# A mixture-of-experts decoder layer on one core: experts placed by token count, 14 of 32 places with 64 slots and two passes over the weights

## The chip, the cores and the metric

The kernel runs on one core of a Trainium2 chip (trn2). The metric is the device time of one execution in microseconds; lower is better. TensorE (PE) multiplies matrices; VectorE (DVE), ScalarE (ACT) and GpSimd (POOL) do the other arithmetic; SyncE (SP) issues most DMA transfers, which run on the core's 16 DMA engines. Every engine works through its own instructions in program order and meets the others at semaphores.

## The reference

One decoder layer for 512 tokens of width 1024, all in float32. Retention, dilated attention and their merge come first and are the same in both kernels. What matters here is the mixture of experts at the end: a softmax router picks 4 of 32 experts for each token, and an expert is a clamped SwiGLU network with weights of 1024 x 2048 and 1024 x 1024.

```python
logits = xf @ w_router + b_router
top_val, top_idx = lax.top_k(logits, 4)
gates = softmax(top_val)
# for each expert e, on the tokens that chose it (xb):
u = xb @ w1[e] + b1[e]
glu = minimum(u[:, ::2], 7.0)
lin = clip(u[:, 1::2], -7.0, 7.0)
a = glu * sigmoid(1.702 * glu) * (lin + 1.0)
y = a @ w2[e] + b2[e]                 # added to the token's row, times its gate
```

The weights of all experts are 32 x 12 MB. 512 x 4 choices over 32 experts are 64 tokens per expert in the mean.

## The kernel before

The mixing half fills the first part of the program. Then the router: for each of four blocks of 128 tokens, `choose` finds the four experts, `count` and `rank` give each token its place in its expert's list (`rk1`), and `gates` writes the gate as three bfloat16 parts into `aux`, beside the token's number.

The expert stage takes the experts in order, e = 0 to 31, each with 96 slots (`CAP`). Weights come as tiles of 1 MB: eight "A" tiles for the first matrix (128 rows of 2048 columns) and four "B" tiles for the second. The list `tiles` has the order: A tiles of e, then the B tiles of e - 1. `load` (L847) issues a tile's DMA from SP into a ring of 11 buffers (`NRA` + `NRB` + `NRC`). A float32 product is made of reduced-precision ones (float32r): `prep_hi` (L1010) has ACT round a weight tile into `w_hi`, `prep_lo` (L1016) has DVE subtract that from the weights into `w_lo`, and then issues the load that reuses the tile's buffer. There are four buffers for `w_hi` and four for `w_lo`, and both run `AHEAD` = 3 tiles ahead of the matmuls in program order. The activations are split the same way into `xh`, `xl`, 96 columns each. A tile then takes three groups of four matmuls, xh by hi, xh by lo, xl by hi, each with 512 columns (L1217 for A, L1232 for B):

```python
for s_, m_ in ((xh, hi), (xh, lo), (xl, hi)):
    for j in range(4):
        PE.matmul(U[e][:, j], s_[:, k], m_[:, j * 512:(j + 1) * 512], start=False, ...)
```

The order of everything else is written out by hand in the loop over `tiles`, at fixed tile numbers k of A(e). `slot_hot` (k = 5, DVE, L1098) and `slot_sum` (k = 7, PE) find the tokens of expert e + 2; `slot_rows` (ACT and POOL) makes their numbers and gathers the rows with an indirect DMA (L1119). `turn` (PE, L1130) transposes the gathered rows of e + 1 at k = 5 and 6, and the activations of e - 1 at k = 3 and 4; `turn_copy` (L1075 ACT, L1076 DVE) splits them. `evacuate`, at the first two B tiles that follow A(e), reads the sums u: `open_gates` (ACT, L1141), `linear` (DVE, L1146), `times_glu` (DVE, L1150). `times_gate` (DVE, L1153) follows at k = 1 of the next A, and `finish` at k = 0 of the one after it: DVE scales y into `ys` (L1158), POOL adds the rows to `s_acc` in HBM with an indirect DMA (L1159). u is one PSUM buffer of four banks, y one of two, so A(e + 1) can't begin before u of e is read. Biases enter by a matmul each (`bias_mm`, L1094).

`overflow_list` writes down which experts have more than 96 tokens; after the 32 places a loop on the chip (L1281) takes one extra pass for each such block. The final norm follows.

Of the kernel before, what the change touches and what calls it, by code (L numbers as in the profile page):

```python
# [27 lines left out]
CAP = 96  # L28
F2 = 2048
# [6 lines left out]
NRB = 2  # L36
# [14 lines left out]
def _constants():  # L51
# [30 lines left out]
    m = np.zeros((P, 324), np.float32)  # L82
# [6 lines left out]
    m[:, 259] = np.arange(P) % 32  # L89
    for p in range(P):  # L90
        m[p, 260 + 32 * (p // 64) + p % 32] = 1.0
# [5 lines left out]
def body(tc, a, out):  # L97
# [14 lines left out]
    misc = cp.tile([P, 324], F32, name="misc")  # L112
# [668 lines left out]
    G.tensor_copy(sel, misc[:, 260:324].rearrange("p (a b) -> p a b", a=2))  # L781
# [65 lines left out]
    loaded, his, los = {}, {}, {}  # L847
# [54 lines left out]
    def choose(t):  # L902
# [29 lines left out]

    def gates(t0, t1):
# [7 lines left out]
        g0, g1 = gt[:, 0, :n], gt[:, 1, :n]  # L941
# [150 lines left out]
    def bias_mm(ps, e, r):  # L1092
        c = (r % 3) * 512
        PE.matmul(ps, sel[:, r // 3, e:e + 1].to_broadcast([P, CAP]), btile[:, c:c + 512], start=True, stop=False)  # L1094

    def slot_hot(rk_e):
        oh = m2.tile([P, NT, CAP], BF, name="oh", bufs=1)
        V.tensor_tensor(oh, iota96[:, None, :].to_broadcast([P, NT, CAP]), rk_e[:, :, None].to_broadcast([P, NT, CAP]),  # L1098
                        op=OP.is_equal)
        return oh  # L1100

    def slot_sum(oh, aux_e):
        ps = psC.tile([CAP, 8], F32, name="psl", tag="pt", bufs=2)
        for t in range(NT):
            PE.matmul(ps[:, :6], oh[:, t], aux_e[:, t], start=(t == 0), stop=(t == NT - 1))
        return ps

    def slot_rows(ps, fetch_rows=True):
        sl = m2.tile([CAP, 10], F32, name="sl")
        A.activation(sl[:, :6], ps[:, :6], AF.Copy)  # L1110
        G.tensor_scalar(sl[:, 6:7], sl[:, 2:3], misc[:CAP, 258:259], misc[:CAP, 257:258], op0=OP.mult, op1=OP.add)  # L1111
        G.tensor_add(sl[:, 7:8], sl[:, 0:1], sl[:, 1:2])
        idx = m2.tile([CAP, 1], I32, name="idx", bufs=4)
# [3 lines left out]
        if fetch_rows:  # L1117
            xg = m2.tile([CAP, D], F32, name="xg", bufs=1)
# [3 lines left out]
        gate = m2.tile([CAP, 1], F32, name="gate", bufs=4)  # L1122
# [21 lines left out]
    def linear(u):  # L1144
        av = m2.tile([CAP, 4, 256], F32, name="av", bufs=1)
# [6 lines left out]
    def times_gate(sg, av):  # L1152
        V.scalar_tensor_tensor(av, sg, top7[:CAP, 1:2], av, op0=OP.min, op1=OP.mult)  # L1153
        return av.rearrange("p a b -> p (a b)")

    def finish(y, gate, idx):
        ys = m2.tile([CAP, D], F32, name="ys", bufs=1)
        V.scalar_tensor_tensor(ys, y.rearrange("p a b -> p (a b)"), gate, gtF[:CAP], op0=OP.mult, op1=OP.mult)  # L1158
        G.indirect_dma_start(out=acc, out_offset=bass.IndirectOffsetOnAxis(ap=idx[:, :1], axis=0), in_=ys,  # L1159
                             in_offset=None, compute_op=OP.add)  # L1160

    def overflow_list():
        pc = psC.tile([E, E], F32, name="pc", tag="pt", bufs=2)
        for t in range(NT):
            PE.matmul(pc, trib[:, 1, :E], selb[:, t], start=(t == 0), stop=(t == NT - 1))
        cn = m1.tile([E, 4, E], F32, name="cn")
        V.tensor_scalar(cn[:, 0], pc, float(CAP), None, op0=OP.is_gt)
        for b in range(2, 6):
# [203 lines left out]
```

## Time and profile before

| | |
|---|---|
| median of 3 runs | 1931.7 us (1931.44 to 1932.92) |
| the profiled execution | 1930.4 us, its span 1928.6 us |
| granted TensorE clock, mean | 0.981 |
| instructions | 23299 |
| loads of weight tiles | 384 of 1 MB, median 8.1 us from issue to landing |
| HBM read, written | 503.35 MB, 19.99 MB |

All times are of one execution taken by the hardware profiler. PE is the row of matmuls, PEld that of weight loads into the array, which overlap matmuls. Matmuls are pipelined, so what counts is the distance from one start to the next, not the length of one. "Idle before" is the time that the engine stood still just before, and behind the arrow stands what ended it. PEclk is the granted share of TensorE's full clock of 2.4 GHz: 0.50 is 1.2 GHz. The letter q behind an engine is its queue of instructions. x12 is a count.

### The profile page before, as it was taken

How to read it: one execution, taken by the hardware profiler on the slowest of the kernel's cores; microseconds unless marked ns; L12 is line 12 of the kernel's file. 1: busy time of each engine (PE TensorE's matmuls, PEld its weight loads, DVE VectorE, ACT ScalarE, POOL GpSimd, SP SyncE). 2: the span in 40 equal slices, each digit the busy share in tenths (PEclk: the TensorE clock that was granted, in tenths of full speed). 3: DMA queues.
4: the chain of work that ended last, by engine and by line, in shares of the span. 5: the costliest groups of instructions: out<-in, count | busy, mean ns of one | idle time of the engine just before them, and what ended most of it. 6: DMA issues, size and time to landing. Idle time of an engine off the chain costs nothing. (4 is left out here: it accounts for less than half of the span.)

```text
span 1928.6 us, 23299 instructions
## 1 busy us (share of the span) xinstructions
PE 1847.5 (96%) x8937; PEld 1381.2 (72%) x8937; DVE 1507.3 (78%) x1489; ACT 1025.8 (53%) x939; POOL 411.9 (21%) x404
## 2 busy tenths in 40 slices
PE   5979999999999979999999999999999999999994
PEld 4868888888778866666766766766766766766662
DVE  7474536567553587999999999999999999999993
ACT  5133323222222336666766766676776676776672
POOL 2140001010110123432222232232232232232201
PEclk8999999999999989999999999999999999999997
DMA  9513334433663848999999999999999999999963
GB/s 313 161 54 101 89 90 141 120 90 94 190 174 110 308 153 319 335 370 366 365 361 373 370 356 373 373 351 379 368 358 367 378 358 369 372 357 373 366 238 104
DMA packets 207650, 524.90 MB, mean 272 GB/s; under 512 B 11974, under 2 KB 127094, under 8 KB 174640
## 3 DMA queue, kind: packets, MB, share of 16 engines
q1 hardware_dynamic: 197024, 492.33, 70.8%
q0 software_dynamic: 10512, 31.06, 6.7%
q8 instruction: 71, 1.16, 0.3%
q14 instruction: 43, 0.35, 0.1%
HBM read 503.35 MB, written 19.99 MB: 271 GB/s over the span
## 5 line engine op out<-in xcount | busy, mean ns | idle before, releaser
L1016 DVE TENSOR_TENSOR w_lo<-w_moe,w_hi 128x2048 fp32r<-128x2048 f32 x384 | 874.6, 2290 | 87.6 <-ACT w_hi L1010 83.7
L1010 ACT ACTIVATE w_hi<-w_moe 128x2048 fp32r<-128x2048 f32 x384 | 736.3, 1918 | 359.8 <-PE u L1217 237.9
L1217 PE MATMUL u<-w_hi,x 128*96 128x512 f32 x2048 | 555.5, 398 | 0.0
L1217 PEld LDWEIGHTS u<-w_hi,x 128*96 128x96 f32 x2048 | 319.1, 162 | 122.2 <-issue 0.5
L1217 PE MATMUL u<-w_lo,x 128*96 128x512 f32 x1024 | 278.2, 393 | 0.0
L1232 PE MATMUL y<-w_hi,at 128*96 128x512 f32 x1024 | 264.5, 396 | 0.0
L1232 PEld LDWEIGHTS y<-w_hi,at 128*96 128x96 f32 x1024 | 165.8, 162 | 72.2 <-ACT at L1075 0.2
L1217 PEld LDWEIGHTS u<-w_lo,x 128*96 128x96 f32 x1024 | 165.1, 161 | 72.0
L1111 POOL TENSOR_SCALAR sl<-sl,misc 96x1 f32<-96x1 f32 x32 | 75.9, 2371 | 502.8 <-ACT sl L1110 502.8
L194 PE MATMUL pp<-hTh,w_hl 128*128 128x512 f32 x400 | 162.1, 405 | 0.0
L195 PE MATMUL pp<-hTl,w_hl 128*128 128x512 f32 x400 | 158.4, 396 | 0.0
L196 PE MATMUL pp<-hTh,w_hl 128*128 128x512 f32 x400 | 158.4, 396 | 0.0
L185 DVE TENSOR_TENSOR w_hl<-w_raw,w_hl 128x1024 fp32r<-128x1024 f32 (+1 forms) x66 | 90.9, 1390 | 74.2 <-ACT w_hl L184 74.2
L1232 PE MATMUL y<-w_lo,at 128*96 128x512 f32 x512 | 140.2, 396 | 0.0
L1159 POOL DMA_INDIRECT s_acc<-ys,idx x32 | 58.3, 1823 | 360.9 <-DVE ys L1158 345.3
L1232 PEld LDWEIGHTS y<-w_lo,at 128*96 128x96 f32 x512 | 83.1, 162 | 36.3
L184 ACT ACTIVATE w_hl<-w_raw 128x1024 fp32r<-128x1024 f32 (+1 forms) x66 | 65.2, 1002 | 73.7 <-PE pp L196 56.2
L194 PEld LDWEIGHTS pp<-hTh,w_hl 128*128 128x128 f32 x400 | 75.4, 188 | 20.1 <-issue 2.2
L196 PEld LDWEIGHTS pp<-hTh,w_hl 128*128 128x128 f32 x400 | 75.3, 188 | 18.4
L195 PEld LDWEIGHTS pp<-hTl,w_hl 128*128 128x128 f32 x400 | 75.4, 189 | 16.6
L259 POOL DMA_DIRECT2D s_mod<-brow x16 | 7.9, 493 | 283.0 <-DVE brow L256 251.9
L226 PE MATMUL pp<-w_hl,hTh 128*128 128x256 f32 x224 | 67.4, 301 | 0.4 <-ACT w_hl L210 0.4
(294 smaller groups left out, 2345.1 us busy)
## 6 DMA issues: line engine op xcount, KB each, us to landing
w_moe<-in_w_mlp SPq DMA_DIRECT2D x384, 1024.0 KB, 8.1
w_raw<-in_w_in SPq DMA_DIRECT2D x76, 512.0 KB, 5.5
w_ada<-in_w_ada SPq DMA_DIRECT2D x24, 1024.0 KB, 5.7
w_raw<-in_w_ret_o SPq DMA_DIRECT2D x8, 512.0 KB, 4.4
w_o<-in_w_o SPq DMA_DIRECT2D x4, 1024.0 KB, 5.1
xin<-in_x SPq DMA_DIRECT2D x4, 512.0 KB, 6.5
w_raw<-in_w_att_o SPq DMA_DIRECT2D x8, 256.0 KB, 4.5
xs<-in_x SPq DMA_DIRECT2D x8, 256.0 KB, 4.8
```

The costliest lines, as they stand in the source:

```text
L184: A.activation(hi[:, :kc], raw, AF.Copy)
L185: eng.tensor_tensor(lo[:, :kc], raw, hi[:, :kc].bitcast(F32), op=OP.subtract)
L194: PE.matmul(ps, hi[:, k], mh[:, k], start=(k == 0), stop=False)
L195: PE.matmul(ps, hi[:, k], ml[:, k], start=False, stop=False)
L196: PE.matmul(ps, lo[:, k], mh[:, k], start=False, stop=(k == kc - 1))
L226: PE.matmul(ps[:, tt], xh, hi, start=(kc == 0), stop=False)
L1010: A.activation(his[i], loaded[i], AF.Copy)
L1016: V.tensor_tensor(los[i], loaded[i], his[i].bitcast(F32), op=OP.subtract)
L1111: G.tensor_scalar(sl[:, 6:7], sl[:, 2:3], misc[:CAP, 258:259], misc[:CAP, 257:258], op0=OP.mult, op1=OP.add)
L1159: G.indirect_dma_start(out=acc, out_offset=bass.IndirectOffsetOnAxis(ap=idx[:, :1], axis=0), in_=ys, in_offset=None, compute_op=OP.add)
L1217: PE.matmul(U[e][:, j], s_[:, k], m_[:, j * 512:(j + 1) * 512], start=False, stop=(k == KC - 1 and s_ is xl))
L1232: PE.matmul(Y[e][:, n], s_[:, 2 * k + c], m_[:, col:col + 512], start=False, stop=(k == 3 and s_ is al and c == 1))
```

## The change

The experts are sorted by their token count on the chip. Experts 0 and 1 keep their places; the other thirty follow in falling order of count, assigned to 18 large places ("L", 96 slots) first and to 14 small ones ("S", 64 slots) after. The places are run in the order `KIND` = "LLLL" + "LS" x 14, so from place 4 on large and small alternate, and the last place is small.

In a small place the high and low parts of the activations lie side by side: 64 + 64 columns are one stationary operand of 128 columns. A weight tile then takes two groups of four matmuls, by hi and by lo, and gives 128 rows of sums: rows 0 to 63 from the high parts, rows 64 to 127 from the low parts. At the end `lower` has ACT copy the lower rows out of PSUM, and `fold` has PE add them to the upper rows, one matmul for each bank against a shifted identity.

The sort is done on PE and DVE during the tiles of expert 0: `sort_counts` at k = 0, `sort_rows` and `sort_turn` at k = 1, `sort_tables` at k = 3. It gives `sorted_i` (which expert is at which place), and `rkp`, `aux` and the selectors of the biases in the order of the places. From place 2 on, SP reads the expert's number from `sorted_i` into a register, and the addresses of the loads come from it. The ring of load buffers has 10 places instead of 11. `evacuate` is done in one step at the first B tile instead of two. `overflow_list` counts by the slots of each place, and the extra loop takes the expert's number from the list.

The diff, cut to its core:

```diff
+SMALL = 64
+KIND = "LLLL" + "LS" * 14
...
-NRB = 2
+NRB = 1
...
+        if kind == "A" and k == 0 and e > 1:
+            which[e] = nc.values_load(sorted_i[0:1, e:e + 1], engines=[mybir.EngineType.SP], min_val=0, max_val=E - 1)
+        at = ds(which[e], 1) if e > 1 else slice(e, e + 1)
         if kind == "A":
-            SP.dma_start(w, dram(w1, (e * D + k * P) * F2, [[F2, P], [1, F2]]))
+            SP.dma_start(w, w1[0, at].rearrange("o (k p) n -> p (o k) n", p=P)[:, k])
         else:
             SP.dma_start(w.rearrange("p (k n) -> p k n", k=2),
-                         dram(w2, (e * D + k * 2 * P) * D, [[D, P], [P * D, 2], [1, D]]))
+                         w2[0, at].rearrange("o (k p) n -> p (o k) n", p=P)[:, 2 * k:2 * k + 2])
...
+        V.tensor_copy(selb[:, t], sel_t[t % 2][:, None, :].to_broadcast([P, 4, E]))
...
+    def gate_parts(g, rest, s):
+        V.tensor_copy(aux[:, :, s, 3], g)
+        V.tensor_tensor(rest, g, aux[:, :, s, 3], op=OP.subtract)
+        V.tensor_copy(aux[:, :, s, 4], rest)
+        V.tensor_tensor(aux[:, :, s, 5], rest, aux[:, :, s, 4], op=OP.subtract)
...
-        V.tensor_tensor(g0, g1, nm[:, 1, :n, None].to_broadcast([P, n, E]), op=OP.mult)
-        V.tensor_copy(aux[:, t0:t1, :, 3], g0)
-        V.tensor_tensor(g1, g0, aux[:, t0:t1, :, 3], op=OP.subtract)
-        V.tensor_copy(aux[:, t0:t1, :, 4], g1)
-        V.tensor_tensor(aux[:, t0:t1, :, 5], g1, aux[:, t0:t1, :, 4], op=OP.subtract)
+        V.tensor_tensor(rg[:, t0:t1, 1], g1, nm[:, 1, :n, None].to_broadcast([P, n, E]), op=OP.mult)
+        if t1 == NT:
+            gate_parts(rg[:, :, 1, 0:2], gt[:, 1, :, 0:2], slice(0, 2))
...
+    def two_parts(t, e):
+        if KIND[e] == "L":
+            t = t.rearrange("p (a k c) -> p a k c", a=2, k=KC)
+            return [t[:, 0], t[:, 1]]
+        both = t[:, :KC * P].rearrange("p (k c) -> p k c", k=KC)
+        return [both[:, :, :SMALL], both[:, :, SMALL:], both]
...
+    def lower(ps):
+        n = ps.shape[1]
+        low = m1.tile([P, 4, 512], F32R, name="low")
+        A.activation(low[SMALL:, :n], ps[SMALL:], AF.Copy)
+        return low
+
+    def fold(ps, low):
+        for j in range(ps.shape[1]):
+            PE.matmul(ps[:SMALL, j], shift[SMALL:], low[SMALL:, j], start=False, stop=True, skip_group_check=True)
...
+    def sort_counts():
+        ps = psC.tile([P, 40], F32, name="cnt", tag="pt", bufs=2)
+        for t in range(NT):
+            PE.matmul(ps[:, 0:1], selb[:, t].rearrange("p a e -> p (a e)"), trib[:, 1, 0:1], start=(t == 0), stop=(t == NT - 1))
+        for t in range(NT):
+            PE.matmul(ps[:, 8:40], trib[:, 1], selb[:, t, 0], start=(t == 0), stop=(t == NT - 1))
+        V.scalar_tensor_tensor(sc_[:, 0:1], ps[:, 0:1], 32.0, misc[:, 264:265], op0=OP.mult, op1=OP.add)
+        V.tensor_copy(sc_[:, 1:2], ps[:, 0:1])
+        V.scalar_tensor_tensor(so[:, 0], ps[:, 8:40], 32.0, misc[:, 299:331], op0=OP.mult, op1=OP.add)
+        V.tensor_scalar(so[:, 1], so[:, 0], sc_[:, 0:1], None, op0=OP.is_gt)
+        V.tensor_reduce(sc_[:, 2:3], so[:, 1], axis=AX.X, op=OP.add)
+        V.tensor_scalar(so[:, 2], misc[:, 267:299], sc_[:, 2:3], None, op0=OP.is_equal)
+        for a_ in range(2):
+            V.tensor_copy(both[E * a_:E * (a_ + 1), a_], so[E * a_:E * (a_ + 1), 2])
+        for a_ in range(2):
+            V.tensor_scalar(sel[:, a_, 2:], so[:, 2, 2:], misc[:, 265 + a_:266 + a_], None, op0=OP.mult)
...
+    def sort_rows():
+        ps = psC.tile([E, 2, E], F32, name="srt", tag="pt", bufs=2)
+        PE.matmul(ps[:, 0], misc[:E, 256:257].to_broadcast([E, E]), so[:E, 2], start=True, stop=True)
+        PE.matmul(ps[:, 1], sc_[:E, 1:2].to_broadcast([E, E]), so[:E, 2], start=True, stop=True)
+        V.tensor_copy(sorted_i, ps[0:1, 0])
+        V.tensor_copy(sq_, ps)
+
+    def sort_turn():
+        ps = psC.tile([2 * E, NT, P], F32, name="rgt", tag="pt", bufs=2)
+        for t in range(NT):
+            PE.transpose(ps[:, t], rg[:, t].rearrange("p a e -> p (a e)"), ident)
+        rgT = m2.tile([2 * E, NT, P], F32, name="rgT", tag="ys", bufs=1)
+        A.activation(rgT, ps, AF.Copy)
+        return rgT
+
+    def sort_tables(rgT):
+        ps = psC.tile([P, NT, 2, E], F32, name="srt2", tag="pt", bufs=2)
+        for t in range(NT):
+            PE.matmul(ps[:, t], rgT[:, t], both, start=True, stop=True)
+        V.tensor_copy(rkp, ps[:, :, 0])
+        V.tensor_copy(rg[:, :, 1], ps[:, :, 1])
+        gate_parts(rg[:, :, 1, 2:], rg[:, :, 0, 2:], slice(2, E))
...
-    def evacuate(e, step):
-        if step == 0:
-            SG[e] = open_gates(U[e])
-            AVS[e] = linear(U[e])
-        else:
-            times_glu(U.pop(e), AVS[e])
+    def evacuate(e):
+        if KIND[e] == "S":
+            fold(U[e], now["low"])
+        u = U.pop(e)[:slots_of(e)]
+        SG[e] = open_gates(u)
+        AVS[e] = linear(u)
+        times_glu(u, AVS[e])
+
+    def close(e):
+        if KIND[e] == "S":
+            fold(Y[e], now["ylow"])
+        finish(Y.pop(e), SL[e][1], SL[e][0])
...
+            if e == 0 and k == 1:
+                sort_rows()
+                rgT = sort_turn()
+            if e == 0 and k == 3:
+                sort_tables(rgT)
...
+            else:
+                for m_ in (hi, lo):
+                    for j in range(4):
+                        PE.matmul(U[e][:, j], X[e][2][:, k], m_[:, j * 512:(j + 1) * 512], start=(k == 0 and m_ is hi),
+                                  stop=False, skip_group_check=True)
+                    if k == 0 and m_ is hi:
+                        for j in range(4):
+                            bias_mm(U[e][:SMALL, j], e, j, False)
...
+            if e == 0 and k == 0:
+                sort_counts()
...
-                finish(Y.pop(e - 2), SL[e - 2][1], SL[e - 2][0])
+                close(e - 2)
...
+            if k == KC - 1:
+                if KIND[e] == "S":
+                    now["low"] = lower(U[e])
+                if e == 0:
+                    evacuate(0)
...
+        else:
+            if e + 1 < E:
+                if k == 0:
+                    evacuate(e + 1)
+                if e + 1 == E - 1 and k == 2:
+                    AVS[e + 1] = times_gate(SG.pop(e + 1), AVS[e + 1])
+                    AT[e + 1] = at_tiles(e + 1)
+            if k == 3:
+                if KIND[e] == "S":
+                    now["ylow"] = lower(Y[e])
+                if e >= E - 2:
+                    close(e)
```

`close` is called for the place before last and the last at the end of their own B tiles. The B tiles of a small place are built like its A tiles, with `AT[e][2]` as the stationary operand.

## Rows read from the trace of the kernel before

**Rows 1.** The page: busy us (share of span), instructions, by engine.

```profile
PE 1847.5 (96%) x8937; PEld 1381.2 (72%) x8937; DVE 1507.3 (78%) x1489; ACT 1025.8 (53%) x939; POOL 411.9 (21%) x404
```

**Rows 2.** Windows, expert stage: us, busy us (count) by engine, PEclk, DMA share, GB/s.

```profile
1100.00:1200.00 100.00, 99.92 (x464) 69.92 (x462) 93.28 (x58) 69.55 (x48) 31.12 (x24) 1.00 1.00 369
```

**Rows 3.** Waits, 900 to 1800 us: waiter, releaser, total us, times, longest.

```profile
ACT w_hi L1010 <- PE u L1217: 180.2, 175, 1.8
...
DVE w_lo L1016 <- ACT w_hi L1010: 60.3, 146, 0.7
```

**Rows 4.** Line 853, a load, 900 to 1800 us: issue to landing.

```profile
DMA to landing us min/median/max: 6.1/8.1/10.9
```

**Rows 5.** Timeline of SP's queue: start us, us, engine, line, operation, names, count.

```profile
971.30 21.00 SPq L853 DMA_DIRECT2D w_moe<-in_w_mlp  x8
...
1007.84 21.01 SPq L853 DMA_DIRECT2D w_moe<-in_w_mlp  x8
```

**Rows 6.** Timeline of PE's weight loads, one B tile, then an A tile.

```profile
1003.42 0.86 PEld L1232 LDWEIGHTS y<-w_lo,at 128*96 128x96 f32 x4
...
1006.20 0.86 PEld L1232 LDWEIGHTS y<-w_lo,at 128*96 128x96 f32 x4
...
1021.96 0.86 PEld L1217 LDWEIGHTS u<-w_lo,x 128*96 128x96 f32 x4
...
1025.08 0.85 PEld L1217 LDWEIGHTS u<-w_lo,x 128*96 128x96 f32 x4
```

**Rows 7.** Timeline of PE's weight loads, stage before the experts.

```profile
691.61 0.19 PEld L833 LDWEIGHTS o<-wo_hl,mg 128*128 128x128 f32 x1
...
691.84 0.19 PEld L834 LDWEIGHTS o<-wo_hl,mg 128*128 128x128 f32 x1
```

**Rows 8.** Groups by shape, one expert (1008.05 to 1044.6): busy us, mean ns, idle before.

```profile
L1016 DVE TENSOR_TENSOR w_lo<-w_moe,w_hi 128x2048 fp32r<-128x2048 f32 x13 | 29.6, 2290 | 2.5 <-ACT w_hi L1010 2.5
...
L1010 ACT ACTIVATE w_hi<-w_moe 128x2048 fp32r<-128x2048 f32 x12 | 23.0, 1918 | 11.1 <-PE u L1217 7.2 <-PE y L1232 2.1 <-DMA w_moe<-in_w_mlp 0.9
...
L1158 DVE SCALAR_TENSOR_TENSOR ys<-y,gate,gtF 96x1024 f32<-96x1024 f32 x1 | 1.3, 1272 | 0.0
...
L1146 DVE TENSOR_SCALAR av<-u 96x1024 f32<-96x1024 f32 x1 | 1.2, 1214 | 0.0
...
L1076 DVE TENSOR_TENSOR x<-pt,x 128x384 fp32r<-128x384 f32 x2 | 1.1, 547 | 0.0
...
L1141 ACT ACTIVATE sg<-u 96x1024 f32<-96x1024 f32 x1 | 1.0, 1001 | 0.0
```

**Rows 9.** Timeline of DVE, start of the first expert.

```profile
714.44 0.27 DVE L944 CAST aux<-gt 128x64 bf16<-128x64 f32 x1
...
716.46 6.69 DVE L1016 TENSOR_TENSOR w_lo<-w_moe,w_hi 128x2048 fp32r<-128x2048 f32 x3
```

**Rows 10.** Timeline of PE: two waits, [idle before <-releaser].

```profile
748.41 1.99 PE L1094 MATMUL u<-btile,selrow 128*96 128x512 f32 x4 [3.84 <-DVE av L1150]
...
1888.20 1.17 PE L1094 MATMUL y<-btile,selrow 128*96 128x512 f32 x2 [4.03 <-DVE ys L1158]
```

**Rows 11.** Windows around them, and one ahead of the first expert.

```profile
747.85:751.26 3.41, 2.85 (x7) 1.99 (x8) 2.61 (x2) 0.00 (x0) 2.82 (x3) 0.50 0.98 359
...
1887.90:1894.73 6.83, 6.53 (x20) 4.60 (x21) 3.08 (x4) 2.78 (x3) 1.43 (x1) 0.50 0.40 59
...
710.30:720.54 10.24, 8.10 (x27) 6.40 (x28) 9.72 (x16) 4.43 (x6) 0.49 (x1) 0.50 0.70 217
```

**Rows 12.** Line 1280: a register read on SP's queue, minimum/median/maximum ns.

```profile
L1280 SPq TENSOR_LOAD <-li x1: 481/481/481, 1862.6 to 1862.6; - x1
...
L1280 SPq FUSED_REGOPS  x1: 181/181/181, 1863.2 to 1863.2; - x1
```

**Rows 13.** A window of 8 us in the expert stage.

```profile
864.00:872.00 8.00, 7.92 (x38) 5.38 (x37) 7.51 (x5) 4.50 (x4) 1.50 (x1) 1.00 1.02 408
```

**Rows 14.** The page, groups: the accumulates of the experts' rows.

```profile
L1159 POOL DMA_INDIRECT s_acc<-ys,idx x32 | 58.3, 1823 | 360.9 <-DVE ys L1158 345.3
```

More of the change, by code (lines that the diff above doesn't have):

```diff
@@ L89, in _constants @@
     m[:, 259] = np.arange(P) % 32
+    e = np.arange(E)
     for p in range(P):
-        m[p, 260 + 32 * (p // 64) + p % 32] = 1.0
+        if p % 32 < 2:
+            m[p, 260 + 2 * (p // 64) + p % 32] = 1.0
+    first = np.where(e == 0, 1e6, np.where(e == 1, 5e5, 0.0)) - e
+    m[:, 264] = first[np.arange(P) % 32]
+    m[:, 265] = np.arange(P) < 64
+    m[:, 266] = np.arange(P) >= 64
+    large = [i for i in range(E) if KIND[i] == "L"]
+    small = [i for i in range(E) if KIND[i] == "S"]
+    rank = np.zeros(E)
+    rank[large + small] = np.arange(E)
+    slots = np.array([CAP if k == "L" else SMALL for k in KIND])
+    m[:, 267:299] = rank[None]
+    m[:, 299:331] = first[None]
+    m[:, 331:363] = slots[None]
+    m[:, 363:394] = np.diff(slots)[None]
     c["k_misc"] = m
@@ L920, in count @@
         for tt in range(t + 1):
-            PE.matmul(pr, trib[:, 0 if tt == t else 1], selb[:, tt], start=(tt == 0), stop=(tt == t))
+            PE.matmul(pr, trib[:, 0 if tt == t else 1], selb[:, tt, 0], start=(tt == 0), stop=(tt == t))
         return pr
@@ L988, in body @@
             load_x(t, n)
+    sorted_i = rt.tile([1, E], I32, name="sorted_i")
     for i in range(NRA + NRB):
@@ L1126, in turn @@
     def turn(rows, q):
+        n = rows.shape[0]
         pt = psC.tile([P, 4, CAP], F32, name="pt", tag="pt", bufs=2)
@@ L1159, in finish @@
+        V.scalar_tensor_tensor(ys, y[:n].rearrange("p a b -> p (a b)"), gate, gtF[:n], op0=OP.mult, op1=OP.mult)
         G.indirect_dma_start(out=acc, out_offset=bass.IndirectOffsetOnAxis(ap=idx[:, :1], axis=0), in_=ys,
                              in_offset=None, compute_op=OP.add)
-    def overflow_list():
[L1163 to L1168, printed above, removed]
-            V.scalar_tensor_tensor(cn[:, 0], pc, float(b * CAP), cn[:, 0], op0=OP.is_gt, op1=OP.add)
+    so = m1.tile([P, 3, E], F32, name="so")
@@ new lines, in body @@
+    sc_ = m1.tile([P, 3], F32, name="sc")
+    sq_ = m1.tile([E, 2, E], F32, name="sq")
+    both = m1.tile([2 * E, 2, E], F32, name="both")
+    G.memset(both, 0.0)
+    def sort_counts():
[14 more added lines that the diff above has]
+            V.tensor_scalar(sel[:, a_, 2:], so[:, 2, 2:], misc[:, 265 + a_:266 + a_], None, op0=OP.mult)
@@ new lines, in sort_tables @@
+    def sort_tables(rgT):
[5 more added lines that the diff above has]
+        gate_parts(rg[:, :, 1, 2:], rg[:, :, 0, 2:], slice(2, E))
+    def overflow_list():
+        cn = m1.tile([E, 5, E], F32, name="cn")
+        V.tensor_sub(cn[:, 4], sq_[:, 1], misc[:E, 331:363])
+        V.tensor_scalar(cn[:, 0], cn[:, 4], 0.0, None, op0=OP.is_gt)
+        for b in range(1, 5):
+            V.scalar_tensor_tensor(cn[:, 0], cn[:, 4], float(b * CAP), cn[:, 0], op0=OP.is_gt, op1=OP.add)
@@ L1211, in body @@
                 U[e] = u_tile()
-                for j in range(4):
-                    bias_mm(U[e][:, j], e, j)
-            xh, xl = X[e]
-            for s_, m_ in ((xh, hi), (xh, lo), (xl, hi)):
-                for j in range(4):
-                    PE.matmul(U[e][:, j], s_[:, k], m_[:, j * 512:(j + 1) * 512], start=False,
-                              stop=(k == KC - 1 and s_ is xl))
+                if KIND[e] == "L":
+                    for j in range(4):
+                        bias_mm(U[e][:CAP, j], e, j)
+            if KIND[e] == "L":
+                xh, xl = X[e]
+                for s_, m_ in ((xh, hi), (xh, lo), (xl, hi)):
+                    for j in range(4):
+                        PE.matmul(U[e][:CAP, j], s_[:, k], m_[:, j * 512:(j + 1) * 512], start=False,
+                                  stop=(k == KC - 1 and s_ is xl))
+            else:
+                for m_ in (hi, lo):
+                    for j in range(4):
+                        PE.matmul(U[e][:, j], X[e][2][:, k], m_[:, j * 512:(j + 1) * 512], start=(k == 0 and m_ is hi),
+                                  stop=False, skip_group_check=True)
+                    if k == 0 and m_ is hi:
+                        for j in range(4):
+                            bias_mm(U[e][:SMALL, j], e, j, False)
         else:
```

175 lines of the change are left out of this document (95 added, 80 removed).

## The prediction

> **What bounds the kernel now.** I read the page first, then the windows, the waits and the expert's own rows. Over the span PE is busy 96% and DVE 78% [rows 1]; the mean hides stages, so the reader should go to 100 us in the middle of the expert stage: PE 99.92, DVE 93.28, ACT 69.55 us, and the DMA engines at a share of 1.00 with 369 GB/s [rows 2]. Three resources look full. The waits tell them apart: ACT's `w_hi` waits for PE to give a buffer back (180.2 us in 900), DVE's `w_lo` waits for ACT (60.3 us) [rows 3], and a load lands 6.1 to 10.9 us after its issue [rows 4], though it is issued eleven weight tiles ahead. So PE sets the pace and the loads are early. One expert lasts 1007.84 - 971.30 = 36.54 us [rows 5], twelve tiles at 3.05, so a load has some 30 us.
>
> Inside it, a tile of 12 matmuls takes 1006.20 - 1003.42 = 2.78 us, 0.2317 us each; a tile with four transposes 1025.08 - 1021.96 = 3.12, so 0.34 for them [rows 6]. 144 + 6 bias matmuls are 34.75 us, four sets of transposes 1.36, and the rest of 36.54, 0.43, is the slot sums.
>
> **The change part by part.** 14 places (e = 5, 7, ... 31; call them S) put the high and low parts of up to 64 tokens side by side as one 128-column stationary. Then two products (hi, lo) replace three: 96 matmuls for 144. Whether 128 columns cost more than 96 shows in the stage before: two weight loads of 128 columns with 512-column matmuls lie 691.84 - 691.61 = 0.23 us apart [rows 7], so no. S adds six `fold` matmuls (four on u, two on y) that contract 64 rows; no row has one. A transpose is 0.09 (0.34 / 4), a 512-column matmul at half clock 0.46; I take 0.2317, the nearest in columns, and the ends are worth 1 us a pair. PE per S place: 108 x 0.2317 + 1.36 + 0.43 = 26.8 us; a pair of L and S 63.3 instead of 73.1.
>
> DVE splits the same weights: 12 `w_lo` at 2.29 us and the vector work on 1024 columns. That takes 1.21 to 1.27 us on 96 partitions, just over half of 2048 columns on 128 [rows 8]: length goes by columns, and 64 partitions save nothing. An L place needs 0.9328 x 36.54 = 34.1 us; in a pair the five small operations of S have a third fewer columns (5 x 0.18 = 0.9 less): 67.3 us. ACT: 25.4 us per L place; S adds `lower`, 2048 columns of u and 1024 of y, 2.0 and 1.0 us by `sg`, which takes 1.00 for 1024 from PSUM [rows 8]; 53.8 per pair. `lower(u)` waits on ACT for the last matmul of k = 7, and behind it stands the `w_hi` of the second B tile: 2.0 + 1.9 us, while DVE still has three `w_lo` (6.7 us) to make, so nobody waits. `fold` stands on PE behind the first B tile and holds the other three for 0.9 us, counted below. So after the change DVE needs more than PE, and the most that a pair can gain is 73.1 - 67.3 = 5.8 us.
>
> It will not get all of that, since the engines follow one program order with four `w_hi` and four `w_lo` buffers. Follow one turn of the loop of waits. `times_gate` of the place before sits on DVE behind `w_lo` of k = 4, and PE can't transpose at k = 3 before it. In an S place PE arrives there early (its first tiles take 1.86 us, DVE's `w_lo` 2.29, and `ys` and `times_gate` stand between), so PE idles. From there PE runs without a stop: five S tiles (40 matmuls), the B tiles of the L place before (50 with bias), the fold of u (4), the next L place's A tiles (100): 194 x 0.2317 = 44.9, eight sets of transposes 2.7, two slot sums 0.9: 48.5 us. At the end of that k = 7 tile a `w_hi` buffer is free: ACT 1.92 us [rows 8]. Then DVE is late: six `w_lo` (three in a row took 6.69 us, 2.23 each [rows 9]) 13.4, the two operations on u at 1.21 and `ys` and `times_gate` at 1.27 [rows 8] (the second of each kind takes the same) 5.0: 18.4 us, to the next `times_gate`. One turn is 48.5 + 1.9 + 18.4 = 68.8 us. L places stay PE-bound, S places become DVE-bound, and the handover costs 1.5 us of the 5.8.
>
> The idle before k = 3 is 5 to 6 us: after the third tile PE has nothing for `w_lo` (2.2), `ys` (1.3) and `times_gate` (1.3) and part of another `w_lo`. The trace has two idle stretches of that kind: PE stands from 744.56 and resumes at 748.41; its granted clock is 0.50 (1.2 GHz) from 747.85 to 751.26. At 1888.20 after 4.03 us it is 0.50 until 1894.73 [rows 10, 11]. So PE runs at half clock for 2.85 and 6.53 us after it resumes and loses 1.4 or 3.3 us. The stretch after the idle is on the turn's path. I take 2.0, nearer to the short case since the idle lies on no other disturbance there; both ends go into the range. A pair then takes 70.8 us and saves 2.3; thirteen pairs (e = 5 to 30) 30 us.
>
> The sort, at the start. `sort_counts`, `sort_rows`, `sort_tables` and the longer `overflow_list` add on DVE about 11 + 2 + 6 + 7 small operations, less about four that `gates` drops there: 22 x 0.2 to 0.27 us, as the small casts there [rows 9], 5 us. On PE some 18 small matmuls and transposes, under 2 us; ACT one copy. In this first expert DVE is late: PE waits 3.84 us for DVE's `av` [rows 10]. So I take nearly all, +4.5; 0 if DVE's slack in the next L places hid it, 8 if PE's new wait for `oh` at k = 1 sets its clock back once more.
>
> The loads: from e = 2 on each address comes from a register. Thirty reads of `sorted_i` on SP's queue; the only such read on SP in the trace takes 0.48 us plus 0.18 of register work [rows 12]. SP issues a load every 3 us at 0.33 us, and a load lands over 20 us before its use, so this hides; were it uncovered, 30 x 0.66 = 20 us. One buffer fewer in the ring (11 to 10) takes about 3 us of that lead: nothing, unless the DMA queue is the limit (a rival). Gather and accumulate move 64 rows for 96. Evacuating u in one step moves `times_glu` one tile earlier, before the next A needs u: nothing.
>
> The end: the last place is S. Its B tiles have 16 matmuls fewer (-3.7 us), with `lower` (1.0) and `fold` (0.5 and handoffs) ahead of the last `ys`, -2; its A tiles save half a pair's gain, -1. Together -3.
>
> The sum goes against the profiled execution, 1930.4 us (span 1928.6; 1.3 below the median of 1931.7): 1930.4 + 4.5 - 30 - 3 = 1902 us.
>
> **The rivals.**
> 1. *DVE alone bounds the pairs*: times_gate's wait is soaked up and PE's clock stays at 1.00. Then 67.3 a pair, 5.8 x 13 = 75: 1930.4 + 4.5 - 75 - 3 = 1857 us. For it: DVE has work all through S. Against: its waits for ACT [rows 3] don't vanish in L places.
> 2. *DMA is at its limit*: share 1.00 at 369 GB/s [rows 2]. A pair moves 73.1 x 369 = 26.97 MB now and 0.26 less after (32 rows x 4 KB, in and out), 72.4 us: 0.7 x 13 = 9: 1922 us. Against it: a window of 8 us in the same stage at 408 GB/s and a share of 1.02 [rows 13], and loads that land 8 us after issue instead of filling their 30 us lead. The pairs as forecast want 26.7 MB in 70.8 us, 377 GB/s, under those 408. Beside it, the Trainium skill ("DMA: Bandwidth & Descriptors", Where 436 GB/s comes from) says that about 358 GB/s of HBM per core binds such loads; by that rule a pair's 25.8 MB of reads would take 72.1 us, a gain of 13 us in all before head and tail, 1919. The window at 408 GB/s speaks against it as a limit here.
> 3. *Slower: PE's clock*. If each S place's idle is followed by a low stretch like that of 10.24 us at 710.30 [rows 11], PE loses 5.1 us a turn: 73.9 a pair, 0.8 x 13 = 10 lost: 1930.4 + 4.5 + 10 - 3 = 1942. It decides from 73.1 - 68.8 = 4.3 us lost, that is 8.6 us at half clock on the path. For it: one such idle comes every pair, and later waits inside S may hold the clock down; against: the two single idle stretches cost 1.4 and 3.3.
> 4. *It doesn't fit*: an S place with over 64 tokens goes to the extra loop, an expert's 12 loads again, at least 36.5 us and nothing hidden: 1902 + 37 = 1939 or more. In the trace the loop never ran: 32 accumulates for 32 experts [rows 14]. From the reference's inputs, experts 0 and 1 get 71 and 54 tokens, the sixteen largest others 66 to 91, the fourteen smallest 40 to 62. So it should fit.
>
> **How the numbers follow.** Forecast 0.57 (own range 1871, no clock loss and no head, to 1922, a clock loss of 3.3 and a head of 8); rival 1 0.13; rival 2 0.12; rival 3 0.13; rival 4 0.05. A measurement of this kernel can tell 0.2%, 4 us, from no change. Faster: nearly all of the forecast, rival 1 and most of rival 2: 0.78. Same: the rest of 2 and the near side of 3: 0.08. Slower: 0.14. The range must take in rival 1's 1857 and rival 2's, and leaves the slower cases out: 1852 to 1932.
>
> **What would show it.** Right: load issues of two places 70 to 72 us apart, the S half shorter than 36.5 and the L half near 36; in S, DVE busy nearly throughout, PE idle 5 us before the transposes of `av` with `times_gate` as releaser, and a granted clock of 0.50 after it; in L, ACT's `w_hi` still waiting for PE. Wrong: `w_hi` waiting for DMA in each pair (rival 2); no clock below 1.00 and 67 us pairs (rival 1); pairs over 73 (rival 3); more than 32 accumulates (rival 4).

## The result: 1909.8 us, 1.2% faster, and the profile after

The changed kernel takes 1909.8 us (median of 4 runs, 1909.71 to 1911.79) where the kernel before took 1932.3 beside it (1931.44 to 1934.36): ratio 0.9884, interval 0.9867 to 0.9902. The profiled execution took 1909.79, its span 1908.0. The forecast was 1902, counted from the profiled 1930.4: 20.6 us were gained where 28.4 were forecast.

The page's engine line and a window of the expert stage, as [rows 1, 2]:

```profile
PE 1754.7 (92%) x8369; PEld 1332.6 (70%) x8369; DVE 1491.2 (78%) x1506; ACT 1052.6 (55%) x968; POOL 463.7 (24%) x406
```

```profile
1100.00:1200.00 100.00, 90.02 (x396) 64.77 (x395) 93.33 (x58) 72.93 (x54) 27.95 (x24) 0.94 1.00 369
```

PE lost ten points in this window, which holds two of its stands (from 1000 to 1100 us, with one, it is busy 95.05); DVE kept its 93, and the DMA row has not moved: the transfers follow the pace of the experts, as e7 below shows. The waits from 900 to 1800 us, as [rows 3], say who is late now:

```profile
ACT w_hi L1039 <- PE u L1339: 109.9, 96, 1.8
...
PEld pt L1175 <- DVE av L1209: 73.3, 25, 5.4
PE pt L1175 <- DVE av L1209: 62.4, 13, 5.0
DVE w_lo L1045 <- ACT w_hi L1039: 59.1, 78, 1.6
```

Thirteen times, once per pair, PE stands ahead of the transposes (L1175) for `times_gate` (L1209). Loads land in a median of 8.1 us as before [rows 4], and 32 accumulates of rows stand in the page as in [rows 14]: no extra pass.

One turn of the loop, in the timeline of one pair (start us, us, engine, line, operation, names, [idle before <-releaser]):

```profile
1483.81 0.90 PE L1175 MATMUL pt<-misc,av 96*128 96x96 f32 x4 [5.00 <-DVE av L1209]
...
1535.40 1.92 ACT L1039 ACTIVATE w_hi<-w_moe 128x2048 fp32r<-128x2048 f32 x1 [1.03 <-PE u L1339]
...
1537.35 2.32 DVE L1045 TENSOR_TENSOR w_lo<-w_moe,w_hi 128x2048 fp32r<-128x2048 f32 x1 [0.71 <-ACT w_hi L1039]
...
1554.18 1.27 DVE L1209 SCALAR_TENSOR_TENSOR av<-sg,top,av 96x1024 f32<-96x1024 f32 x1
...
1555.50 0.90 PE L1175 MATMUL pt<-misc,av 96*128 96x96 f32 x4 [5.01 <-DVE av L1209]
```

PE takes 1535.40 - 1483.81 = 51.59, ACT 1.95, DVE 1555.45 - 1537.35 = 18.10, the handover 0.05: 71.69 us. No row of that chain has idle time inside its part. The clock behind one of the stands (window; PE resumes at 979.94):

```profile
979.94:986.07 6.13, 6.13 (x19) 4.98 (x20) 6.13 (x4) 2.89 (x3) 0.12 (x1) 0.50 1.04 371
```

Where the 20.6 us of the spans went is seen in the start of the first A matmul of a place, beside the kernel before and one more (e8 below: before with its constant tile widened):

```
us                            before   e8 (padded)   after
first A matmul                 718.0      714.7      711.9
places 0 and 1                  70.5       72.6       76.4
A(2)                           788.5      787.3      788.4
A(5)                           899.6      898.2      899.3
A(31)                         1849.3     1845.5     1829.7
13 pairs, A(5) to A(31)        949.7      947.3      930.4
span                          1928.6     1923.4     1908.0
```

Nearly all lies in the pairs: 73.05 became 71.57. A pair has two halves: 39.1 us from the first A matmul of the small place to that of the large one, and 32.6 from there to the next small one.

### The profile page after: what moved, and what is told of

Read it like the earlier page. It is cut to its first block, busy times and chain, and to the rows that moved or that the text cites. A ratio compares the mean times of both kernels' runs of the same rounds, so it can differ in the third digit from the quotient of the medians.

```text
span 1908.0 us, 23014 instructions
## 1 busy us (share of the span) xinstructions
PE 1754.7 (92%) x8369; PEld 1332.6 (70%) x8369; DVE 1491.2 (78%) x1506; ACT 1052.6 (55%) x968; POOL 463.7 (24%) x406
## 3 DMA queue, kind: packets, MB, share of 16 engines
q1 hardware_dynamic: 197024, 492.36, 71.4%
## 5 line engine op out<-in xcount | busy, mean ns | idle before, releaser
L1339 PE MATMUL u<-w_hi,x 128*96 128x512 f32 x1152 | 315.8, 401 | 0.0
L1339 PEld LDWEIGHTS u<-w_hi,x 128*96 128x96 f32 x1152 | 180.3, 163 | 72.1 <-issue 0.2
L1339 PE MATMUL u<-w_lo,x 128*96 128x512 f32 x576 | 156.9, 394 | 0.0
L1364 PE MATMUL y<-w_hi,at 128*96 128x512 f32 x576 | 151.3, 396 | 0.0
L1344 PE MATMUL u<-w_hi,x 128*128 128x512 f32 x448 | 141.1, 440 | 0.0
L1344 PE MATMUL u<-w_lo,x 128*128 128x512 f32 x448 | 130.6, 417 | 0.0
L1364 PEld LDWEIGHTS y<-w_hi,at 128*96 128x96 f32 x576 | 91.7, 161 | 44.4 <-issue 5.9
L1344 PEld LDWEIGHTS u<-w_lo,x 128*128 128x128 f32 x448 | 91.5, 204 | 22.5
L1175 PE MATMUL pt<-misc,av 96*128 96x96 f32 (+1 forms) x256 | 37.0, 274 | 70.9 <-DVE av L1209 70.9
L1344 PEld LDWEIGHTS u<-w_hi,x 128*128 128x128 f32 x448 | 85.8, 207 | 19.6 <-issue 5.4
L1175 PEld LDWEIGHTS pt<-misc,av 96*128 96x128 f32 (+1 forms) x256 | 28.6, 163 | 94.0 <-DVE av L1209 82.9
L211 PEld LDWEIGHTS pp<-hTh,w_hl 128*128 128x128 f32 x400 | 75.5, 189 | 18.0 <-issue 2.6
```

The lines of the kernel that those rows point to most:

```text
L211: PE.matmul(ps, hi[:, k], mh[:, k], start=(k == 0), stop=False)
L1175: PE.transpose(pt[:, i, :n], rows[:, c * P:(c + 1) * P], ident[:n, :n])
L1339: PE.matmul(U[e][:CAP, j], s_[:, k], m_[:, j * 512:(j + 1) * 512], start=False, stop=(k == KC - 1 and s_ is xl))
L1344: PE.matmul(U[e][:, j], X[e][2][:, k], m_[:, j * 512:(j + 1) * 512], start=(k == 0 and m_ is hi), stop=False, skip_group_check=True)
L1364: PE.matmul(Y[e][:CAP, n], s_[:, 2 * k + c], m_[:, col:col + 512], start=False, stop=(k == 3 and s_ is al and c == 1))
```

## The experiments

Theory: the loop of waits through `times_gate` sets 71.7 us. Rivals: DVE's 67.3 us of work as such; the DMA engines (a share of 1.00 before and after). Ratios are to the kernel before, on the same chip; *after* has 0.9884.

**e1, e2: the two parts of the loop.** In e1 `times_gate` runs earlier, at k = 1 of the B tiles instead of k = 1 of the next A tiles; in e2 PE does work whose result nobody reads before the transposes of a small place. The first two pieces of the diff are e1, the last is e2.

```diff
-            if e and k == 1:
-                AVS[e - 1] = times_gate(SG.pop(e - 1), AVS[e - 1])
+            if e == 1 and k == 1:
+                AVS[0] = times_gate(SG.pop(0), AVS[0])
...
+                if k == 1:
+                    AVS[e + 1] = times_gate(SG.pop(e + 1), AVS[e + 1])
...
+            if KIND[e] == "S" and k == 3:
...
+                for _ in range(24):
+                    PE.matmul(d, trib[:, 0], selb.rearrange("p t a e -> p (t a e)")[:, :4 * CAP], start=True, stop=True)
```

> The product with the gate (times_gate) moves from k = 1 of the next A to the second B tile, so that PE need not stand before the transposes at k = 3. Theory (one turn of the loop of waits: 48.5 us of PE work, 1.9 of ACT, 18.4 of DVE, and PE at half clock after its 5 us stand): the turn is cut, the stand and the low clock go, and DVE's own work sets a pair, 67.0 to 67.3 us instead of 71.7, so 13 x 4.5 = 58 us less: about 1852 us, PE's granted clock at 1.00 in the pairs. Rival, the DMA engines are at their limit at 370 to 377 GB/s: a pair moves 26.7 MB and stays at 71 to 72 us, so 1898 to 1910, with w_hi waiting for the loads.

> Order as in the changed kernel; in each small place 24 matmuls of 384 bf16 columns, whose result nobody reads, stand on PE ahead of the transposes at k = 3, where it waits 5 us for times_gate. They keep it busy and change no wait. Theory: the stand still lasts until times_gate, but the clock stays at 1.00, so only the loss at half clock goes (6.1 of 6.8 low us lie in work, 3.1 us a pair): 68.6 us a pair, 13 x 3.1 = 40 us less, about 1870 us. Rival (DVE or the DMA engines set the pair, the low clock is hidden): 1908 to 1912, or later if the added matmuls outlast the wait.

e1: 1907.6 us (0.9872, 0.9856 to 0.9889). e2: 1902.6 (0.9845, 0.9829 to 0.9861), the fastest median of the kernels that do the whole work. Both stay far above the 1852 and 1870 that the theory gave. In e1 the wait for `av` is gone from the list and another has its place (waits from 1000 to 1788 us, 11 pairs):

```profile
PEld pt L1175 <- DVE at L1117: 45.2, 11, 4.1
...
POOL idx L1159 <- DMA s_acc<-ys,idx: 44.8, 11, 5.3
...
PE pt L1175 <- DVE at L1117: 40.4, 11, 3.7
```

There are two PSUM buffers for transposes, and the subtraction (L1117) that frees one stands on DVE behind the `w_lo` of its tile. In e2 the window 1100 to 1200 has a clock of 1.00, yet the halves are 38.8 and 32.6: of 3.1 us lost to the clock per turn 0.3 came back. PE then waits in four places, a little in each, and the first two rows show where ACT and DVE take over ahead of it:

```profile
1460.74 1.92 ACT L1039 ACTIVATE w_hi<-w_moe 128x2048 fp32r<-128x2048 f32 x1 [1.03 <-PE u L1343]
...
1462.69 2.31 DVE L1045 TENSOR_TENSOR w_lo<-w_moe,w_hi 128x2048 fp32r<-128x2048 f32 x1 [0.71 <-ACT w_hi L1039]
...
1480.84 0.55 PE L1175 MATMUL pt<-misc,av 96*128 96x96 f32 x4 [1.08 <-DVE av L1209]
...
1485.71 0.55 PE L1175 MATMUL pt<-misc,xg 96*128 96x96 f32 x4 [0.22 <-DVE at L1117]
...
1488.38 0.55 PE L1175 MATMUL pt<-misc,xg 96*128 96x96 f32 x4 [0.23 <-DVE at L1117]
...
1491.37 0.26 PE L1148 MATMUL psl<-aux,oh 128*64 128x6 bf16 x4 [0.60 <-DVE x L1117]
```

The wait at 1491.37 closes a second loop. The same wait stands one turn earlier, at 1419.97. From there PE works without a stop until ACT's `w_hi` starts at 1460.74 (40.77 us); ACT takes 1.95; and DVE works without a gap from 1462.69 to the subtraction into `x` that PE's `slot_sum` waits for (28.68 us, to 1491.37). That is 71.40 us, the pair of e2, with the clock at full. So the loop through `times_gate` is one of several of nearly the same length, which share DVE's full stretch in the small place.

**e3, e4: the places.** `KIND` is `"L" * 32`, and `"L" * 18 + "S" * 14`.

> All 32 places large (96 slots, three products), still sorted by count with the loads' addresses from a register and a ring of 10 buffers: the sort and its costs without the small places. Theory: places last 36.5 us as before; the sort's 6 us of longer first expert are met by the 6 us that the stage ahead of the experts is shorter in the trace of the changed kernel, so 1930 us, within 3 of the kernel before. Rival (register addresses or the smaller ring cost something in each place, 0.5 us or more): 1946 or more. Rival (the sort is free): 1925.

> Same places, other order: 18 large ones first, then 14 small ones in a row instead of in turn. Theory: large places stay at PE's 36.5 us; in a row of small places PE has 26.8 us of work and its stand and low clock cost nothing, so DVE's 33.2 to 33.4 us set the place: 36.5 + 33.3 = 69.8 for what is a pair now at 71.7, 13 x 1.9 = 25 us less, about 1885 us. Rival (the DMA engines' limit at 370 to 377 GB/s): a small place moves 13.1 MB and takes 34.8 to 35.4 us, so 1903 to 1913.

e3: 1926.0 (0.9966, 0.9952 to 0.9980), 36.4 us a place. Against e8 below (the kernel before with the same wide constant tile, 1924.0) sort, registers and the smaller ring cost some 2 us in all, which the spread of the two (1922.5 to 1927.6) hardly tells from nothing, and nothing in a place. e4: 1917.0 (0.9928, 0.9911 to 0.9944): above both expectations; a small place among small ones takes 36.1 us, which with 13.1 MB is 363 GB/s. By itself that speaks for the DMA rival. The trace speaks against it: from 1500 to 1780 us a load lands in a median of 7.4 us, no engine waits for one from 1480 on, and PE stands 49.8 us in nine places for `times_gate`, once in each small place. From 1500 to 1700 DVE is busy 182.2 of 200 us and the clock is at 0.91. Which chain of links adds up to the 36.1 was not worked out.

**e7: DVE against the DMA engines.** `w_lo` is made of half the columns, and its matmuls read these twice; the low parts of the other half of the weights are left out. The loads are the same.

```diff
-        V.tensor_tensor(los[i], loaded[i], his[i].bitcast(F32), op=OP.subtract)
+        los[i] = los[i][:, :1024]
+        V.tensor_tensor(los[i], loaded[i][:, :1024], his[i][:, :1024].bitcast(F32), op=OP.subtract)
```

> The kernel after with w_lo made of the first 1024 of 2048 columns only, and the matmuls reading these twice: this leaves out the low parts of half of the weights' columns; loads, w_hi and matmuls are as they were. It takes 12 x 1.13 = 13.6 us of DVE's work off each expert. Order and lookahead theories alike: DVE has 40 us of work per pair, the wait ahead of the transposes goes (chain 68.8 - 6 x 1.13 = 62), and the pair falls to the PE's 63.3 to 65: 1910 - 14 x 7.5 = 1805 (1795 to 1825; the four large experts at the start hardly gain). DMA rival: 71 to 71.7 per pair as before, 1900 to 1910.

1826.0 us (0.9436, 0.9419 to 0.9453). The first half falls from 39.1 to 33.2 in places 7 to 20, the second stays at 32.6. A window of it, the time from a load's issue to its landing (900 to 1780 us), and a wait of ACT that is new (1000 to 1788):

```profile
1000.00:1200.00 200.00, 197.24 (x909) 139.68 (x908) 128.55 (x128) 159.88 (x116) 41.86 (x48) 1.00 1.02 394
```

```profile
DMA to landing us min/median/max: 7.9/19.7/24.1
```

```profile
ACT w_hi L1039 <- DMA w_moe<-in_w_mlp: 21.1, 29, 1.8
```

The same engines moved 394 GB/s against 369, so the DMA limit falls as the cause in *after*. This is also how a true approach to that limit looks: landing goes from 8 to 20 us and ACT begins to wait for loads. In *after* neither is seen, though the share is 1.00 there and 1.02 here. In e7 the limit is in fact reached. From place 21 on (1419 us) the first half grows to between 33.9 and 35.3 us, loads land 19 to 24 us after their issue, and 18.6 of the 21.1 us that ACT waits for loads lie behind 1450 us. These last five pairs take 67.1 us in the mean, at 395 GB/s. A pair of *after* moves 369 x 71.57 = 26.4 MB; at 395 GB/s that would be some 67 us, an estimate, where it took 71.57.

**e5, e6, e9: the order on DVE and the lookahead.** On top of e1, e5 issues both copies out of the transposes' buffer ahead of their tile's `w_hi` and `w_lo` (the added lines below; they stood behind `prep_lo`). e6 is *after* with `AHEAD` = 4: a fifth buffer each for `w_hi` and `w_lo`, two fewer in the ring of loads. e9 has both.

```diff
+            if e and k in (3, 4):
...
+                turn_copy(now["at", k - 3], slice(4 * (k - 3), 4 * (k - 3) + 4), AT[e - 1])
+            if e + 1 < E and k in (5, 6):
...
+                turn_copy(now["xt", k - 5], slice(4 * (k - 5), 4 * (k - 5) + 4), X[e + 1])
         prep_hi(i + AHEAD)
         prep_lo(i + AHEAD)
```

> As e1 (times_gate one place earlier), and in each tile of the first matrix the two copies out of pt (ACT copy and DVE subtraction into at and x) are issued ahead of that tile's w_hi and w_lo instead of behind them. Order theory: in e1 the PE stands 3.7 to 4.1 us once per pair for the pt buffer that the subtraction into at releases, which had stood behind w_lo; one w_lo is 2.27 us, so the stand falls by that, 71.7 to 69.4 us per pair, 14 pairs: 1907.6 - 14 x 2.3 = 1875 (1868 to 1885). Lookahead theory (DVE is busy through the whole small place and what is moved ahead of a w_lo only delays that w_lo): little, 1900 to 1908, and PE waits for w_lo in place of pt. DMA rival (13.1 MB per expert at 365 GB/s is 35.9 us): 1905 to 1910.

> The kernel after with w_hi and w_lo made four tiles ahead of their matmuls instead of three: each gets a fifth buffer, taken from the ring of weight loads, which falls from ten to eight. Lookahead theory: large places go by PE (39 us) with DVE waiting for w_hi, small ones by DVE; one tile more of lead lets DVE do one w_lo (2.27) more of the small place's work during the large one, and the lower rates of the clock go with the stand: 71.7 to 68.5 to 69.5 per pair, 1910 - 14 x 2.7 = 1872 (1865 to 1882). The order theory gives much the same (the chain loses one tile of the large place, 2.8 to 3.1 us): 1866 to 1872. DMA rival: loads lead their readers by 6 us less and the transfers stay the limit: 1908 to 1925.

> e5 and e6 together: times_gate one place earlier, the copies out of pt ahead of their tile's w_lo, and w_lo four tiles ahead. Theory (DVE works through the small place without a gap and PE waits for it; in the large place DVE waits 0.2 to 0.7 us per tile for w_hi, because w_hi's buffers come free with PE; e6 alone moved nothing since its chain, too, starts from the buffer that the tile before frees, and times_gate stood behind six w_lo as before): with the gate out of the way the fifth buffer lets DVE go into the small place one large tile, 2.3 to 2.8 us, further ahead; the 38.8 of the pair's second half in e5 falls to 36.0 to 36.5, the 32.6 (PE's own) stays: 1905 - 14 x 2.5 = 1870 (1862 to 1880). Rival: the lookahead is worth nothing, as in e6, and something else holds the 38.8: 1900 to 1908.

e5: 1909.0 (0.9882, 0.9854 to 0.9911). e6: 1913.4 (0.9893, 0.9875 to 0.9911). e9: 1908.1 (0.9882, 0.9863 to 0.9900). All three are misses of the theory: the halves are 38.8 and 32.6 in e5 and e9, 39.1 and 32.6 in e6. I had e6 wrong: with `AHEAD` and the buffers both one more, `w_hi` still takes the buffer that the tile just before frees, and DVE's order is the same, so no link gets shorter. In e5 the wait went on to `slot_sum`'s for `oh`, which is the second loop of e2 with `oh` in the place of `x`, and the same 71.4 us a pair (waits 1000 to 1788):

```profile
PEld L1148 <- DVE oh L1140: 25.5, 11, 3.2
PEld pt L1175 <- DVE at L1117: 22.4, 13, 1.9
```

**e10: less work for DVE.** As e9, with `ys` made by ACT (times gate) and POOL (times gtF).

> As e9, and ys = y x gate x gtF, one DVE instruction of 1.27 us per place, is split: ACT multiplies by gate out of PSUM, POOL by gtF. If DVE's work bounds the small place, 1.27 less in it (and 1.27 less in the large one, where it is of no use): 1870 - 14 x 1.3 to 2.5 = 1835 to 1852. Rival: in the trace POOL's one-column operations take 0.19 us or around 2 us, as if they waited for a w_lo of DVE (2.27) to end; a POOL product of 96x1024 then either starts late, or holds DVE up for its own time (128x512 took 1.41, so some 2.8 for 1024 columns): 1870 to 1900.

1923.2 us (0.9951, 0.9934 to 0.9967), worse than its rival's range. POOL's product took 5.32 us in the mean (windowed groups), and the first half grew to 39.8: what was moved to POOL did not come back as time.

**e11, e12: the remaining links.** e11 is e5 with `oh` at k = 2 instead of 5; in e12 the transposes go to k = 2, 3 (at) and 4, 6 (x) as well.

```diff
-    hot_at.update({(e, 5): e + 2 for e in range(E - 2)})
+    hot_at.update({(e, 2 if e else 5): e + 2 for e in range(E - 2)})
```

> As e5, and oh (DVE, 0.4 to 0.55 us), which slot_sum reads at k=7, is made at k=2 instead of k=5, ahead of three w_lo. Theory (a family of loops through one saturated stretch of DVE): in e5 PE goes 40.7 us without a stop from the slot_sum of a small place to the release of w_hi's buffer near the end of the next large one, ACT takes 1.95 for w_hi, and DVE works 28.6 without a gap from the w_lo behind it to the end of oh, which the next slot_sum waits for: 71.3. With oh ahead of three w_lo the next late thing in that stretch is the subtraction into x, whose pt buffer the slot_sum takes, at 1488.4 in place of 1491.0: 71.4 - 2.5 = 68.9 per pair, 1905 - 14 x 2.5 = 1870 (1864 to 1880). Rivals: DVE and PE each bound their half as such (PE 32.6 in the one, DVE's work and waits 38.8 in the other) and the place of one instruction of 0.5 us is nothing: 1900 to 1908; the DMA engines: the same.

> As e11, and the transposes into pt are moved in the tiles of the first matrix: those for at from k=3 and 4 to k=2 and 3, those for x from k=5 and 6 to k=4 and 6, so that DVE's subtractions stand ahead of one w_lo more before PE needs their buffers again. Theory: every link from DVE back to PE is then shorter than DVE's own work, and what is left is that work, 67.3 us per pair by the forecast's count: 67.4 to 68.5 per pair, 1905 - 14 x 3.3 = 1859 (1850 to 1870). Rival (halves): 1900 to 1908. If the gathered rows or the gate come too late for the earlier transposes, PE waits on POOL's gather or on av instead: 1880 to 1910.

e11: 1958.2 (1.0096, 1.0064 to 1.0128). e12: 2037.7 (1.0545, 1.0524 to 1.0566). Both are slower than the kernel before, outside every range written down. The first half did get shorter (37.4 and 36.7), but the second grew from 32.6 to 38 to 41 in most pairs of e11, and to some 45.5 in most of e12. The timeline of e11, DVE, POOL and PE:

```profile
1514.28 20.87 POOL L1216 DMA_INDIRECT s_acc<-ys,idx  x1 [12.48 <-DVE ys L1215]
...
1527.14 6.67 DVE L1045 TENSOR_TENSOR w_lo<-w_moe,w_hi 128x2048 fp32r<-128x2048 f32 x3
...
1533.74 1.21 DVE L1202 TENSOR_SCALAR av<-u 64x1024 f32<-64x1024 f32 x1
1534.70 17.12 POOL L1155 TENSOR_SCALAR sl<-sl,misc 64x1 f32<-64x1 f32 x1
...
1539.51 6.68 DVE L1045 TENSOR_TENSOR w_lo<-w_moe,w_hi 128x2048 fp32r<-128x2048 f32 x3
...
1555.65 3.02 POOL L1163 DMA_INDIRECT xg<-s_h,idx  x1 [0.56 <-POOL idx L1159]
...
1565.85 0.44 PE L1175 MATMUL pt<-misc,xg 64*128 64x64 f32 x2 [9.65 <-DMA xg<-s_h,idx]
```

A scatter that POOL issued in 3.1 us in *after* (mean from 1000 to 1788 us) takes 20.9, and a one-column operation 17.1, while DVE works without a gap; the first ends at 1535.15, just behind the DVE operation at 1533.74 that reads PSUM. The gather issued at last at 1555.65 brings its rows too late, and PE stands 9.65 us; in e12, with x wanted a tile earlier, PE waits for gathered rows 104.8 us in ten pairs, as its second rival said, though for more than that allowed. POOL's late turns are the cost here. That DVE's pauses are what POOL needs is read from these rows; no run put a pause back to test it. The Trainium skill ("SBUF — State Buffer", Who interferes with whom) has the rule: a DVE instruction with two SBUF inputs, as `w_lo` is, and a GpSimd instruction that reads SBUF exclude one another for a whole instruction. The rows agree (POOL's one-column operations take 0.19 us or some 2.3, one `w_lo`), and go beyond it: through a gapless run POOL was held for some eight `w_lo`. Two things limit this reading. Scatters held for 19 us, once a pair, stand already in e1, e5 and e9 (10.1 us in the mean of all), and PE waits for no gathered row there. And in *after* the scatter issued at 1552.33 us is through in 3.28, though DVE has no gap from 1537.35 on. Which operations of DVE let POOL in was not found out.

**e8: the addresses.** The kernel before with its constant tile `misc` 395 columns wide instead of 324, as in *after*, and no other change.

> The kernel before with its constant tile misc widened from 324 to 395 columns, as the change has it, and nothing else: all tiles allocated behind it move by 284 bytes per partition. In the trace of after the PE's pitch in the unchanged work ahead of the experts is 227 ns where it is 234 ns before, and PE is 4.8 us earlier at 638 us. If the addresses do it: 1926 to 1928 and a pitch of 227 ns at 600 to 640 us. If it is something else (the run, the chip): 1931 to 1933 and 232 to 234 ns.

1924.0 us (0.9945, 0.9927 to 0.9963): faster by 0.5% with not one instruction changed. The window from 400 to 600 us, in which both kernels run the same code, of before, e8 and *after*:

```profile
400.00:600.00 200.00, 199.15 (x949) 159.12 (x948) 120.89 (x240) 48.56 (x66) 17.93 (x33) 1.00 0.48 137
```

```profile
400.00:600.00 200.00, 199.30 (x966) 162.57 (x965) 124.48 (x244) 50.20 (x67) 17.93 (x33) 1.00 0.49 138
```

```profile
400.00:600.00 200.00, 199.29 (x966) 162.58 (x965) 123.75 (x243) 50.23 (x67) 17.98 (x33) 1.00 0.48 137
```

PE fits 966 matmuls where 949 went, at the same clock. All kernels here with the wider tile, *after* and its variants, have 963 to 966. An expert of the kernel before falls from 36.54 to 36.44.

## Why the prediction was right, and what it missed

- *The loop.* Right, term by term: PE's part 48.5 by the forecast and 51.6 measured with the clock's loss in it, ACT 1.9 and 1.95, DVE 18.4 and 18.1; a stand of 5.0 us where 5 to 6 was said, with the releaser named. Of the halves it said the wrong one would be short: counted by A matmuls, the half that begins with the small place's A tiles is the long one, since PE stands in it. By the issue of loads, too, it is 36.6 against 35.1 in the later pairs.
- *The clock.* The term mis-sized: 2.0 forecast, but 6.13 us at 0.50 cost 3.1, near the longer of the two stretches of [rows 11].
- *The next loop.* A pair takes 71.6 instead of 70.8. On 13 pairs that is 10 us, and it is the miss: 19.3 gained for 30. The clock's size explains little of it, since e2, with the clock at full, got 0.3 us a pair back, not 3.1. The forecast followed the one loop that ends last and did not price the one through `slot_sum`, 71.4 us in e2. With that loop in place a pair would have taken 71.4 even with the forecast clock loss of 2.0; so by e2 some 0.6 of the 0.8 us belong to the loop left out, and 0.2 to the clock.
- *The sort.* 4.5 forecast. Places 0 and 1 grew by 5.9 against before, by 3.8 against e8. It did not show at A(2), since the work ahead of the experts ran faster: part of that is the moved addresses (first A matmul 3.3 us earlier in e8 alone), the other 2.8 stays unexplained. In the variants of *after* the first A matmul comes between 709.8 and 713.6, so part of it can be spread.
- *The tail.* -3 forecast, 79.3 to 78.3 measured: a third of it.
- *DVE alone (rival 1).* Not reached by any order tried here. e7 shows that DVE's work makes the first half long, and in e11 and e12 POOL's gather comes too late while DVE has no pause. Whether 67.3 us can be reached with the gather made earlier or issued by another queue was not tried; the last pairs of e7 show that the transfers would bind at about the same length.
- *The DMA limit (rival 2).* Its 369 GB/s was demand: e7 moved 394. By the Trainium skill ("DMA: Bandwidth & Descriptors", Where 436 GB/s comes from) 358 GB/s of HBM per core would bind; e7's weights alone, 24 tiles of 1.049 MB in 65.75 us a pair, are 383, and 375 in its last five pairs, where ACT waits for loads; the measurement decides.
- *Slower (rival 3) and the extra loop (rival 4).* The clock lost 3.1 of the 4.3 us from which it would have decided; no extra pass ran.
- *What belongs to the change.* Against e8 the spans differ by 15.4 us and not 20.6, and the two ratios to before give 0.9884 / 0.9945 = 0.994: something between a quarter and a half of the gain comes from the wider constant tile, which the forecast did not think of. That the time came within 8 us of the forecast is in part luck: without those 5 us the gain of the change itself is 15.4 where 28.4 were forecast.

The next improvement measured is small: e2's 1902.6 us beats both kernels.

## What to carry to other kernels

When a wait is removed, work out the next link of the same chain before counting its gain: here the links through one saturated stretch of DVE came as a family, a few tenths of a microsecond apart. A DMA share of 1.00 did not tell demand from limit here; look whether landing times grow and whether anyone waits for a load. Compare a change also with the kernel before whose tiles lie at the changed addresses.

## What the runs showed of the hardware that was not expected

- PE's pace depends on where tiles lie: 966 against 949 matmuls in the same 200 us of code after a shift of 284 bytes per partition. Which operand's address matters was not tried.
- POOL's one-column operations (0.2 to 2.4 us in the kernel before) and its scatter issues (1.6 us in the mean there) stretch to 17 and 21 us in e11 while DVE works without a gap. The same kind of hold cost nothing in e1, e5 and e9, where the gather still came in time.
- On this core alone on its chip, the weights came at 375 GB/s and all traffic at 395 when the transfers had become the limit (e7).
